# Expert lookup of a diffusion block: dots and sums of the gathered tokens in alternating groups of eight, and the dense tokens' routing earlier

## The chip, the cores and the metric

One Trainium2 chip, of which the program uses one core. The metric is device time in microseconds (us): 1965.21 us, the median of 3 runs (1963.86 to 1965.46). All data are float32.

## The reference, cut to what matters

The program is one layer of a diffusion backbone over 256 latent tokens of width 2048. After the mixers comes an expert feed-forward (PEER): every token picks 8 x 16 = 128 of 16,384 experts by two product keys, takes the dot of itself with each expert's row of `u_tab`, and sums the experts' rows of `v_tab` with gated weights.

```python
def peer_ffn(h, wq, keys, u_tab, v_tab):
    q = (ht @ wq).reshape(n, PEER_HEADS, 2, PEER_DK // 2)
    s = jnp.einsum('nhpc,pkc->nhpk', q, keys)
    s1, i1 = lax.top_k(s[:, :, 0], PEER_TOPK)
    s2, i2 = lax.top_k(s[:, :, 1], PEER_TOPK)
    cand = (s1[..., :, None] + s2[..., None, :]).reshape(n, PEER_HEADS, 256)
    sc, ci = lax.top_k(cand, PEER_TOPK)
    e = i1[ci // 16] * N_KEYS + i2[ci % 16]     # take_along_axis, shortened
    gate = jax.nn.softmax(sc, axis=-1)
    ...
        a = jnp.einsum('nd,nhkd->nhk', xb, jnp.take(u_tab, eb, axis=0))
        w = (gb * jax.nn.gelu(a)).astype(xb.dtype)
        return jnp.einsum('nhk,nhkd->nd', w, jnp.take(v_tab, eb, axis=0))
```

## The kernel before

The expert part treats the tokens in two ways. For 192 dense tokens (`NA`) the products with all 16,384 experts are computed on TensorE, in 128 steps of 128 experts; the wanted ones are picked afterwards. The other 64 gathered tokens (`NB`), two blocks of 32, have their own `u` rows fetched: one gather (an indirect DMA issued on POOL, 128 rows of 8 KB, 1 MB) brings 4 of a token's 128 experts for all 32 tokens of a block, so a block has 32 gathers of `u` rows and 32 of `v` rows. This makes 128 gathers. The dense tokens need 192 more, of `v` rows, after the dense stage: those are the tail.

**The dense stage.** A step loads 1 MB of `u_t` (SP), in two units of 1024 columns. Each unit is split by ACT into `hi` and by DVE into the rest `lo` (three buffers each, so that up to three units are prepared ahead), and TensorE does 8 pairs of matmuls `ups<-hf,hi` (384 columns) and `ups<-hf,lo` (192 columns). At the end of a step ACT copies `ut` out of PSUM and DVE adds it into the tile `W` (one `W<-ut,ups` on DVE is one step done). A `u_t` load needs a free wide buffer (the `wides` list).

**Gathered work beside it.** `gen_gather` walks a list `ops`. A `u` operation is a dot on DVE (`SCALAR_TENSOR_TENSOR ...<-...,hB`, 128x2048, with the sum in a column of `aB`), a `v` operation a sum on TensorE (four matmuls in the order, eight in the trace, into `adaps` for block 0 and `yb` for block 1, with weights `wB` that ACT scales). `fin` makes the weights out of the dots (GELU on ACT, times the gate on DVE); `hB` reloads one buffer with block 1's tokens from DRAM. Gathers are fetched in the list's order whenever a buffer of the list `gaths` is free. Buffers are lent out of `W`, whose later rows are not written yet: pieces 4, 6 and 8 of it for gathers, 1, 2, 3, 5, 7 and 9 for `u_t`, each taken back some steps before its row comes (piece i holds rows from 2048 i / 192 on). Pieces 10 and 11 hold the dense tokens' scores (`s0`) and scratch (`scr`).

**Order.** The code is written out unit by unit; after each one `pump()` advances side work ("lanes") whose due time in a model clock has come: a gather operation every `GP` = 4.65 us of that clock, and the lane `score` with the routing of block 1 of 128 tokens (it holds the gathered ones), a pause of `RT_DELAY`, and the routing of block 0 (dense tokens only): eight `score_top` (two top-16 searches each), four `pair_top`, the lookups `gen_look`, then `gen_route`. At step `RT_AT`, `open_px` completes what is left of that lane, forms the dense tokens' gather indices `eA`, and opens one more wide buffer and one more gather buffer in the space that the routing's tiles leave. Each engine executes its own list in order; only semaphores tie them.

Lines in the profile: every DVE and ACT instruction shows L132, every matmul L353 except the transposes `it` of the routing (L1276), gathers L1362, `u_t` loads L267, the reload of `hB` L1413.

Of the kernel before, what the change touches and what calls it, by code (L numbers as in the profile page):

```python
# [40 lines left out]
NK = 128  # L41
# [33 lines left out]
NA2 = 2  # L75
ADAY = 20.0
LAG = 3.0
UTB = 3
RT_AT = 104
RT_DELAY = 170.0  # L80
GP = 4.65
NAF = 2
GY = 8.0
# [94 lines left out]
def build(tc, a, stack, dbg=None):  # L178
# [851 lines left out]
    gaths = Slots(lambda u: u.used, 2048)  # L1030

    LENT_U = (1, 2, 3, 5, 7, 9)
    LENT = (4, 6, 8)
    x1d = tc.dram_tile([P, KD, T], F32, name="x1_spill")

    def make_hf(u):
        drain(only=("ada",))
        x1 = Y["x"]
        ss = mm_ps("ss1")
        mm(ss[:, 0:T], ones, Y["sq"], start=True, stop=False)  # L1040
        mm(ss[:, 0:T], ones, Y["last"], start=False, stop=True)
        prepare()
        rs = con.tile([P, T], F32, name="rs1", tag="rs1")
        rstd_of(rs, ss[:, 0:T], D)
        araws.drop(V["B"])
        close_pool(V["pb"])
        R["rh"] = open_pool("rh", side="right")
        R["rsb"] = open_pool("rsb", side="right")
        R["rs"] = open_pool("rs", side="right")
        H, S, SB = R["rh"][1], R["rs"][1], R["rsb"][1]  # L1050
        hf = H.tile([P, KD, 2, T], F32R, name="hf", tag="hf")
        hB = H.tile([P, D], F32, name="hB", tag="hB")
        R.update(hB=hB, hf=hf, hfs=hf.rearrange("p k s t -> p s k t"))
        R["keys"] = S.tile([P, 2, NK], F32, name="keys")
        sync.dma_start(R["keys"], a["keys"])
        sync.dma_start(x1d, x1)
        dump("x1", x1)
        n2 = 2 * PH * TOPK
        R["val"] = SB.tile([P, 2, n2], F32, name="val")
        R["ix"] = SB.tile([P, 2, n2], U32, name="ix")  # L1060
        R["sc"] = SB.tile([P, PH, TOPK], F32, name="sc")
        R["ci"] = SB.tile([P, PH, TOPK], U32, name="ci")
        R["e12"] = SB.tile([P, 3, PH, TOPK], F32, name="e12")
        R["h64"] = S.tile([P, KD, NB], F32, name="h64")
        shift, hm = mod[:, 3, 0], {}

        def scaled(k):
            hm[k] = S.tile([P, T], F32, name="hm1", tag="hm1", bufs=4)
            vec.scalar_tensor_tensor(hm[k], x1[:, k], gm[:, 2, k:k + 1], rs, op0=OP.mult, op1=OP.mult)

        skew(KD, scaled,
             lambda k: act.activation(hf[:, k, 0], hm[k], AF.Identity, bias=shift[:, k:k + 1]),
             lambda k: vec.scalar_tensor_tensor(hf[:, k, 1], hm[k], shift[:, k:k + 1],
                                                hf[:, k, 0].bitcast(F32), op0=OP.add, op1=OP.subtract))
        spawn("hA", copy_hB())

        close_pool(pa)
        R["w"] = open_pool("w")
        R["W"] = R["w"][1].tile([P, NK, NA], F32, name="W")
        flat = R["W"].rearrange("p e n -> p (e n)")  # L1080
        room = [flat[:, c * 2048:(c + 1) * 2048] for c in range(NK * NA // 2048)]
        R["scr"] = room.pop()
        R["s0"] = room.pop().rearrange("p (h k) -> p h k", k=NK)
        for i in LENT_U:
            wides.place(("row", i), room[i], i * 2048 // NA - 3)
        for i in LENT:
            gaths.place(("lent", i), room[i])

    hBd = tc.dram_tile([P, D], F32, name="hB_spill")
# [143 lines left out]
    def gen_route(blk, rp):  # L1233
        if blk == 1:
            it = con.tile([P, 1152], F32, name="iT", tag="st")
            R["iT"] = it[:, 0:3 * T].rearrange("p (s t) -> p s t", s=3)
            R["eA"] = it[:, 3 * T:3 * T + NA].bitcast(I32)
            R["idx"], R["gB"], R["aB"] = (
                it[:, c:c + 2 * STEPS].rearrange("p (b s) -> p b s", b=2)
                for c in range(3 * T + NA, 1152, 2 * STEPS))  # L1240
            R["idx"] = R["idx"].bitcast(I32)
            ib = con.tile([P, 2 * T], BF16, name="ib", tag="rs1")
            R["i1b"], R["idb"] = ib[:, 0:T].rearrange("p (b c) -> p b c", b=2), ib[:, T:T + P]
            vec.tensor_copy(R["idb"], ident)
        yield from gen_look(blk, 1, rp)
        sc, e12 = R["sc"], R["e12"]
        sm, e = R["scr"][:, 0:PH], R["scr"][:, 16:16 + P]

        vec.tensor_copy(sm, sc[:, :, 0])
        vec.tensor_tensor(sc, sc, sm[:, :, None].to_broadcast([P, PH, TOPK]), op=OP.subtract)  # L1250
        act.activation(sc, sc, AF.Exp)
        e12f = e12.rearrange("p s h j -> p s (h j)")
        if blk == 1:

            lo = P - NB
            vec.scalar_tensor_tensor(e[lo:P], e12f[lo:P, 0], float(NK), e12f[lo:P, 1], op0=OP.mult, op1=OP.add)
            for g in range(2):
                for r in range(REP):
                    vec.tensor_copy(R["idx"][r * BT:(r + 1) * BT, g],
                                    e[lo + g * BT:lo + (g + 1) * BT, r * STEPS:(r + 1) * STEPS])  # L1260
            spawn("gather", gen_gather())
        vec.tensor_copy(R["i1b"][:, blk], e12f[:, 0])
        yield 1.0
        vec.tensor_reduce(sm, sc, axis=mybir.AxisListType.X, op=OP.add)
        vec.reciprocal(sm, sm)
        vec.tensor_tensor(e12[:, 2], sc, sm[:, :, None].to_broadcast([P, PH, TOPK]), op=OP.mult)
        dump(f"e12_{blk}", e12f)
        if blk == 1:
            for g in range(2):
                for r in range(REP):  # L1270
                    vec.tensor_copy(R["gB"][r * BT:(r + 1) * BT, g],
                                    e12f[P - NB + g * BT:P - NB + (g + 1) * BT, 2, r * STEPS:(r + 1) * STEPS])
        yield ITY
        pt = sm_ps("it")
        for s in range(3):
            ten.transpose(pt[:, s * P:(s + 1) * P], e12f[:, s], ident)  # L1276
        act.activation(R["iT"][:, 0:3, blk * P:(blk + 1) * P], pt[:, 0:3 * P].rearrange("p (s t) -> p s t", s=3),
                       AF.Copy)
        yield 0.0
# [40 lines left out]
    def open_px(u):  # L1320
# [6 lines left out]
        wides.add(R["px"][1], "raw", F32, 1)  # L1327
        gaths.add(R["px"][1], "gath", F32, 1)

    for i, tag in enumerate(("rawA", "rawB")):  # L1330
        wides.take_over(pipe, tag, lambda i=i: all(s[3] is None or raws.done(s[3]) for s in raws.slots[2 * i:2 * i + 2]))
    add(None, False, open_w)
# [49 lines left out]
    def gen_gather():  # L1382

        aB, n = R["aB"], STEPS
        ops = [("u", 0, s) for s in range(n)] + [("fin", 0, 0), ("v", 0, 0), ("hB", 1, 0), ("v", 0, 1)]
        for s in range(n):
            ops += [("u", 1, s)] + [("v", 0, s + 2)] * (s + 2 < n)
        ops += [("fin", 1, 0)] + [("v", 1, s) for s in range(n)]
        for kind, b, s in ops:
            if kind in ("u", "v"):  # L1390
                to_get.append((a[kind + "_rows"], R["idx"][:, b, s:s + 1]))
        scaled = {}

        def scale(b, s):
            w = scaled[b, s] = R["t"][1].tile([P, BT], F32, name="wB", tag="wB", bufs=2)
            act.activation(w, selb, AF.Copy, scale=aB[:, b, s:s + 1])

        fetch()
        yield 4.0
        for j, (kind, b, s) in enumerate(ops):  # L1400
            if kind == "v" and b == 1 and s == 0:
                to_get.extend((a["v_rows"], R["eA"][:, t:t + 1]) for t in range(NA))
            if kind == "fin":
                act.activation(aB[:, b], aB[:, b], GELU)
                vec.tensor_tensor(aB[:, b], aB[:, b], R["gB"][:, b], op=OP.mult)
                YB[b] = ada_ps() if b == 0 else sm_ps("yb")
                yield 2.0
                scale(b, 0)
                yield 2.0
                continue  # L1410
            if kind == "hB":
                R["hB"] = R["rh"][1].tile([P, D], F32, name="hB", tag="hB")
                sync.dma_start(R["hB"], hBd)  # L1413
                continue
            fetch()
            g = got.popleft()
            if kind == "u":
                vec.scalar_tensor_tensor(g.raw, g.raw, 1.0, R["hB"], op0=OP.mult, op1=OP.mult,
                                         accum_out=aB[:, b, s:s + 1])
                g.used = True  # L1420
            else:
                add_rows(YB[b], scaled.pop((b, s)), g, s == 0, s == n - 1)
                if s + 1 < n:
                    scale(b, s + 1)
            fetch()
            yield GP
# [312 lines left out]
```

## Time and profile before

| | |
|---|---|
| median of 3 runs | 1965.21 us |
| the profiled execution's own time | 1964.57 us |
| its span, first to last instruction | 1962.8 us |
| TensorE busy, mean granted clock | 1724.8 us (88%), 0.943 |
| VectorE (DVE) busy | 1224.6 us (62%) |
| ScalarE (ACT) busy | 700.6 us (36%) |
| GpSimd (POOL) busy | 376.6 us (19%) |
| moved by DMA | 670.20 MB, mean 341 GB/s |

Times inside the program are counted from the span's start. The dense stage's 128th step ends at about 1451 us; the stretch from 834 us (14 steps done) to there is what the change touches, and the tail runs from there to 1962.8 us. A busy share is an average over stages, so the stage's own windows are read first, and then what ended the waits in them. TensorE's matmuls are pipelined: it counts as busy also where it runs at the lower clock.

### The profile page before, as it was taken

To read this page: it belongs to the slowest core of one execution; us is meant where nothing else is said; L and a number is where in the kernel's file an instruction comes from. 1 tells how busy PE (TensorE), PEld (TensorE's weight loads), DVE (VectorE), ACT (ScalarE), POOL (GpSimd) and SP (SyncE) were. 2 spreads that over 40 slices of the span, in tenths; PEclk is the share of its full clock that TensorE was granted. 3 is DMA by queue.
4 is the path that set the end of the run, shared out by engine and by line. 5 is a ranking of instruction groups with operands and counts; after the bars stand their busy time and mean duration, and the time that the engine had idled before them with its cause. 6 is when DMAs were issued, how large, how long until landed. Compare 5 with 4: busy or idle time off the path is not lost.

```text
span 1962.8 us, 29973 instructions
## 1 busy us (share of the span) xinstructions
PE 1724.8 (88%) x11882; PEld 1362.9 (69%) x11882; DVE 1224.6 (62%) x2492; ACT 700.6 (36%) x1099; POOL 376.6 (19%) x324
## 2 busy tenths in 40 slices
PE   4999999999899999899899998999987666776775
PEld 2689789879798898899888887888853222222221
DVE  5256868776798669899689996764434323323232
ACT  4235335555543544455444443444421001001000
POOL 0000000000000000333222322223333333333331
PEclk8999999999899999999999999999998998889886
DMA  9975878776698764999999999899989999999996
GB/s 396 368 272 183 287 240 306 275 250 208 198 334 297 262 202 137 422 420 420 373 367 390 387 395 350 338 382 406 380 343 421 421 421 421 421 420 421 420 421 282
DMA packets 115869, 670.20 MB, mean 341 GB/s; under 512 B 12688, under 2 KB 15248, under 8 KB 53264
## 3 DMA queue, kind: packets, MB, share of 16 engines
q1 hardware_dynamic: 69648, 332.72, 45.9%
q0 software_dynamic: 46080, 335.56, 41.7%
q8 instruction: 93, 1.52, 0.3%
q14 instruction: 48, 0.39, 0.1%
HBM read 662.99 MB, written 5.24 MB: 340 GB/s over the span
## 4 chain that ended last, share of the span: by engine, by line
PE 60%; DMA 27%; issue 7%; DVE 4%; ACT 1%; POOL 1%; SPq 0%; POOLq 0%; ACTq 0%; DVEq 0%
PE mm L353 25%; PE ups L353 22%; DMA gath<-in_v_rows,iT 14%; DMA hB<-in_v_rows,iT 2%; PE y L353 2%; PE adaps L353 2%; DMA rawB<-in_v_rows,iT 2%; DMA rawA<-in_v_rows,iT 2%; DMA ring<-in_ada 2%; DMA raw<-in_v_rows,iT 2%; PE sm L353 1%; PE num L353 1%; PE yb L353 1%; DVE lo L132 1%; DMA rawA<-in_u_t 1%
## 5 line engine op out<-in xcount | busy, mean ns | idle before, releaser
L353 PE MATMUL ups<-hf,hi 128*128 128x384 f32 x2048 | 605.3, 368 | 0.0
L353 PE MATMUL ups<-hf,lo 128*128 128x192 f32 x2048 | 516.9, 252 | 16.5 <-DVE lo L132 16.5
L353 PEld LDWEIGHTS ups<-hf,hi 128*128 128x128 f32 x2048 | 389.0, 190 | 51.6 <-issue 43.6
L353 PEld LDWEIGHTS ups<-hf,lo 128*128 128x128 f32 x2048 | 395.6, 193 | 19.3 <-DVE lo L132 19.1
L132 DVE TENSOR_TENSOR lo<-rawA,hi 128x1024 fp32r<-128x1024 f32 x146 | 178.3, 1221 | 118.3 <-ACT hi L132 103.8
L132 DVE TENSOR_TENSOR lo<-rawB,hi 128x1024 fp32r<-128x1024 f32 x144 | 175.7, 1222 | 111.1 <-ACT hi L132 105.0
L132 DVE SCALAR_TENSOR_TENSOR oh<-c,iT,pick 128x128 f32<-128x128 f32 x192 | 55.3, 344 | 298.8 <-PE pick L353 298.8
L1362 POOL DMA_INDIRECT gath<-in_v_rows,iT x134 | 157.1, 1172 | 321.0 <-PE y L353 125.8
L132 ACT ACTIVATE hi<-rawA 128x1024 fp32r<-128x1024 f32 x146 | 154.2, 1056 | 173.1 <-PE ups L353 79.0
L1362 POOL DMA_INDIRECT W<-in_u_rows,iT x28 | 45.1, 1611 | 872.4 <-DMA W<-in_u_t 781.5
L132 ACT ACTIVATE hi<-rawB 128x1024 fp32r<-128x1024 f32 x144 | 152.0, 1057 | 155.1 <-PE ups L353 65.0
L353 PE MATMUL mm<-xL,hi 128*128 128x256 f32 x864 | 181.1, 290 | 4.8 <-ACT xL L132 1.7
L132 ACT ACTIVATE hi<-W 128x1024 fp32r<-128x1024 f32 x106 | 112.4, 1060 | 148.5 <-PE ups L353 143.3
L353 PEld LDWEIGHTS mm<-xL,hi 128*128 128x128 f32 x864 | 144.0, 192 | 14.2 <-issue 7.5
L132 DVE SCALAR_TENSOR_TENSOR adacc<-araw,early,adacc 128x1024 f32<-128x1024 f32 x120 | 152.3, 1277 | 0.0
L353 PE MATMUL y<-gath,wA 128*32 128x512 f32 x648 | 100.6, 701 | 56.7 <-DMA gath<-in_v_rows,iT 56.7
L132 ACT ACTIVATE uA<-uA 128x4 f32<-128x4 f32 x48 | 9.9, 205 | 385.7 <-DVE oh L132 385.7
L132 DVE TENSOR_TENSOR lo<-W,hi 128x1024 fp32r<-128x1024 f32 x106 | 128.4, 1218 | 23.5 <-ACT hi L132 23.1
L353 PE MATMUL mm<-xL,lo 128*128 128x256 f32 x432 | 122.5, 284 | 0.0
L353 PEld LDWEIGHTS pick<-W,oh 128*128 128x128 f32 x384 | 79.4, 255 | 57.8 <-issue 56.3
L353 PE MATMUL mm<-hf,hi 128*128 128x256 f32 x512 | 98.1, 290 | 6.7 <-ACT hf L132 5.3
L353 PE MATMUL pick<-W,oh 128*128 128x128 f32 x384 | 97.9, 412 | 0.7 <-issue 0.7
(278 smaller groups left out, 2871.8 us busy)
## 6 DMA issues: line engine op xcount, KB each, us to landing
araw<-in_ada SPq DMA_DIRECT2D x128, 512.0 KB, 5.1
W<-in_u_t SPq DMA_DIRECT2D x53, 1024.0 KB, 9.4
rawB<-in_u_t SPq DMA_DIRECT2D x34, 1024.0 KB, 9.2
rawA<-in_u_t SPq DMA_DIRECT2D x34, 1024.0 KB, 9.7
ring<-in_ada SPq DMA_DIRECT2D x32, 1024.0 KB, 12.1
rawB<-in_wout SPq DMA_DIRECT2D x16, 512.0 KB, 5.8
rawA<-in_wout SPq DMA_DIRECT2D x16, 512.0 KB, 6.1
rawB<-in_wq SPq DMA_DIRECT2D x16, 512.0 KB, 4.0
```

What stands on the lines that cost most here:

```text
L132: return f(*args, **kw)
L353: ten.matmul(out, lhsT, rhs, start=start, stop=stop, skip_group_check=True, **kw)
L1362: pool.indirect_dma_start(out=g.raw, out_offset=None, in_=tab, in_offset=bass.IndirectOffsetOnAxis(ap=idx, axis=0))
```

## The change

The list `ops` is ordered anew. Before: all 32 dots of block 0, `fin`, its sums mixed with block 1's dots, `fin`, block 1's sums. Now, in each block: dot `s` followed by sum `s - 8`, a `fin` for eight columns after every eighth dot, the last eight sums at the block's end. `hB` is reloaded after the second of block 0's last eight sums. `fin` waits in the model for the gates. The dense tokens' routing starts after 60 instead of 170 us of the model's clock, and `open_px` stands at step 66 instead of 104. It now also lends pieces 10 (to `u_t`, until row 103) and 11 (to gathers, taken back before row 117). The counts of dots, sums, gathers and loads stay; there are 8 `fin` instead of 2.

```diff
+SUB = 8
-RT_AT = 104
-RT_DELAY = 170.0
+RT_AT = 66
+RT_DELAY = 60.0
...
-    LENT = (4, 6, 8)
+    LENT = (4, 6, 8, 11)
...
-        R["scr"] = room.pop()
-        R["s0"] = room.pop().rearrange("p (h k) -> p h k", k=NK)
+        R["room"], R["scr"] = room, room[11]
+        R["s0"] = room[10].rearrange("p (h k) -> p h k", k=NK)
...
-        for i in LENT:
+        for i in LENT[:-1]:
...
+            R["gates"] = True
...
+        wides.place(("row", 10), R["room"][10], 10 * 2048 // NA - 3)
+        gaths.place(("lent", 11), R["room"][11])
...
-        ops = [("u", 0, s) for s in range(n)] + [("fin", 0, 0), ("v", 0, 0), ("hB", 1, 0), ("v", 0, 1)]
-        for s in range(n):
-            ops += [("u", 1, s)] + [("v", 0, s + 2)] * (s + 2 < n)
-        ops += [("fin", 1, 0)] + [("v", 1, s) for s in range(n)]
+        ops = []
+        for b in range(2):
+            for s in range(n):
+                ops += [("u", b, s)] + [("v", b, s - SUB)] * (s >= SUB)
+                if s % SUB == SUB - 1:
+                    ops.append(("fin", b, s + 1 - SUB))
+            ops += [("v", b, s) for s in range(n - SUB, n)]
+
+        ops.insert(ops.index(("v", 0, n - SUB)) + 2, ("hB", 1, 0))
...
-            if kind == "v" and b == 1 and s == 0:
+            if kind == "v" and b == 1 and s == n // 2:
...
-                act.activation(aB[:, b], aB[:, b], GELU)
-                vec.tensor_tensor(aB[:, b], aB[:, b], R["gB"][:, b], op=OP.mult)
-                YB[b] = ada_ps() if b == 0 else sm_ps("yb")
+                while "gates" not in R:
+                    yield 1.0
+                some = slice(s, s + SUB)
+                act.activation(aB[:, b, some], aB[:, b, some], GELU)
+                vec.tensor_tensor(aB[:, b, some], aB[:, b, some], R["gB"][:, b, some], op=OP.mult)
+                if s == 0:
+                    YB[b] = ada_ps() if b == 0 else sm_ps("yb")
                 yield 2.0
-                scale(b, 0)
-                yield 2.0
+                scale(b, s)
+                yield 0.0
...
-                if s + 1 < n:
+                if (s + 1) % SUB:
                     scale(b, s + 1)
```

Three places show what this does to the engines' lists. The first is SP, the queue of the loads, where `hB` is reloaded; numbers in names grow in the order in which the program was written out. Before:

```order
L267 DMA rawA_9180<-in_u_t 128x2048
L267 DMA W_5949<-in_u_t 128x2048 x3
L267 DMA rawB_9376<-in_u_t 128x2048
L1413 DMA hB_9418<-hB_spill_96 128x2048
L267 DMA rawA_9432<-in_u_t 128x2048
```

Now:

```order
L268 DMA rawB_10744<-in_u_t 128x2048
L268 DMA rawA_10799<-in_u_t 128x2048
L1427 DMA hB_10817<-hB_spill_96 128x2048
L268 DMA W_5949<-in_u_t 128x2048
L268 DMA raw0_10900<-in_u_t 128x2048
```

Before, the last dot that reads the old `hB` stands in step 39 of DVE's list, the reload in step 41, the first dot with the new one in step 42. Now they stand in steps 60, 64 and 69, with block 0's last sums between.

The second is DVE, where the dense tokens' `score_top` (MAX, MAX_INDEX, MATCH_REPLACE) meets a dot (`...,hB`). Before, steps 46 and 47:

```order
L132 TENSOR_TENSOR lo_9578<-W,hi_9576 128x1024
L132 MAX val<-W 128x8 x2
L132 MAX_INDEX ix<-val,W 128x8 x2
L132 MATCH_REPLACE W<-val,W 128x128 x2
L132 MAX val<-W 128x8 x2
L132 MAX_INDEX ix<-val,W 128x8 x2
L132 TENSOR_TENSOR lo_9617<-rawB,hi_9615 128x1024
L132 TENSOR_TENSOR W<-ut,ups 128x192
L132 TENSOR_TENSOR lo_9641<-rawB,hi_9639 128x1024
L132 SCALAR_TENSOR_TENSOR gath_9451,iT<-gath_9451,hB 128x2048
L132 TENSOR_TENSOR lo_9666<-rawA,hi_9664 128x1024
```

Now, step 20:

```order
L133 TENSOR_TENSOR lo_8365<-rawA,hi_8363 128x1024
L133 TENSOR_TENSOR W<-ut,ups 128x192
L133 MAX val<-W 128x8 x2
L133 MAX_INDEX ix<-val,W 128x8 x2
L133 MATCH_REPLACE W<-val,W 128x128 x2
L133 MAX val<-W 128x8 x2
L133 MAX_INDEX ix<-val,W 128x8 x2
L133 SCALAR_TENSOR_TENSOR gath_8161,iT<-gath_8161,hB 128x2048
L133 TENSOR_TENSOR lo_8402<-rawA,hi_8400 128x1024
L133 TENSOR_TENSOR lo_8424<-W,hi_8422 128x1024
```

The search and the dot stood two `lo` apart; now they stand side by side between two `lo`, in steps 20, 22, 24, 26 and 28, and a `pair_top` beside a dot in 38, 40 and 42. In the other steps a `lo` stays between.

The third is DVE at the end of the dense tokens' routing, where `e` (gates) is what TensorE's `it` transposes. Before, steps 94 to 96:

```order
L132 COPY W<-sc 128x8
L132 TENSOR_TENSOR sc<-sc,W 128x128
L132 CAST ib<-e_5879 128x128
L132 SCALAR_TENSOR_TENSOR gath_12121,iT<-gath_12121,hB 128x2048
L132 TENSOR_TENSOR lo_12232<-rawB,hi_12230 128x1024
L132 TENSOR_TENSOR W<-ut,ups 128x192
L132 TENSOR_REDUCE W<-sc 128x8
L132 RECIPROCAL W<-W 128x8
L132 TENSOR_TENSOR e_5879<-sc,W 128x128
L132 TENSOR_TENSOR lo_12259<-rawB,hi_12257 128x1024
```

Now, between steps 65 and 66:

```order
L133 TENSOR_REDUCE e_5879<-W 128x64
L133 TENSOR_TENSOR W<-ut,ups 128x192
L133 COPY W<-sc 128x8
L133 TENSOR_TENSOR sc<-sc,W 128x128
L133 CAST ib<-e_5879 128x128
L133 TENSOR_REDUCE W<-sc 128x8
L133 RECIPROCAL W<-W 128x8
L133 TENSOR_TENSOR e_5879<-sc,W 128x128
L133 SCALAR_TENSOR_TENSOR iT<-iT 128x192
L133 TENSOR_TENSOR lo_10905<-W,hi_10903 128x1024
```

`open_px` writes the whole rest of the routing out at one place. On TensorE the transposes `it` stood after step 95, more than a unit behind `e`; now they stand right after step 65's last matmul.

## Rows read from the trace of the kernel before

**Rows 1.** Windows: stretch, length, PE, PEld, DVE, ACT, POOL busy (count), clock, DMA share, GB/s.
```profile
834.00:952.20 118.20, 118.20 (x827) 118.20 (x826) 117.83 (x126) 60.67 (x79) 38.05 (x23) 1.00 1.01 420
952.20:1000.60 48.40, 41.46 (x270) 36.34 (x269) 28.89 (x46) 19.43 (x30) 9.81 (x8) 0.89 0.89 355
1000.60:1164.00 163.40, 163.40 (x1140) 147.38 (x1139) 153.06 (x351) 76.94 (x111) 44.99 (x32) 1.00 0.96 385
1164.00:1320.80 156.80, 144.97 (x971) 128.53 (x970) 108.63 (x132) 67.34 (x99) 38.04 (x28) 0.97 0.93 359
1320.80:1451.50 130.70, 130.70 (x911) 104.77 (x910) 58.63 (x66) 55.57 (x91) 42.58 (x25) 1.00 0.95 373
1451.50:1962.80 511.30, 353.57 (x2196) 136.86 (x2192) 160.68 (x728) 41.28 (x90) 183.36 (x194) 0.85 0.98 407
```

**Rows 2.** Windows, tile ut on DVE: the count is of steps done.
```profile
750.00:834.00 84.00, 4.83 (x14) 0.96 0.75 300
952.20:1000.60 48.40, 2.43 (x7) 0.89 0.89 355
1000.60:1164.00 163.40, 11.05 (x32) 1.00 0.96 385
1164.00:1320.80 156.80, 9.00 (x26) 0.97 0.93 359
1320.80:1451.50 130.70, 7.99 (x23) 1.00 0.95 373
```

**Rows 3.** Windows, tile wB on TensorE: matmuls of the sums, eight to a sum.
```profile
952.20:1000.60 48.40, 5.04 (x32) 0.89 0.89 355
1000.60:1164.00 163.40, 17.05 (x128) 1.00 0.96 385
1164.00:1320.80 156.80, 16.20 (x112) 0.97 0.93 359
1320.80:1451.50 130.70, 27.54 (x208) 1.00 0.95 373
```

**Rows 4.** Timeline of TensorE around 1005 us: start, length, instruction.
```profile
1004.98 0.25 PE L353 MATMUL ups<-hf,lo 128*128 128x192 f32 x1
...
1007.27 0.25 PE L353 MATMUL ups<-hf,lo 128*128 128x192 f32 x1
```

**Rows 5.** The chain of waits in 952:1000.5: start, length, what.
```profile
959.83 14.62 DMA hB<-hB_spill
```

**Rows 6.** Who waited for whom, 1164:1320.8: total, times, longest.
```profile
ACT hi L132 <- DMA rawB<-in_u_t: 21.0, 7, 7.2
...
PE adaps L353 <- DMA gath<-in_v_rows,iT: 10.4, 5, 4.5
```

**Rows 7.** Timeline of DVE around a score_top and a dot.
```profile
1001.53 0.48 DVE L132 MAX8 val<-W 128x8 f32<-128x128 f32 x2
...
1003.88 1.21 DVE L132 TENSOR_TENSOR lo<-W,hi 128x1024 fp32r<-128x1024 f32 x1
1005.00 0.35 DVE L132 TENSOR_TENSOR W<-ut,ups 128x192 f32<-128x192 f32 x1
...
1007.12 2.28 DVE L132 SCALAR_TENSOR_TENSOR W<-W,hB 128x2048 f32<-128x2048 f32 x1
```

**Rows 8.** Groups by line and shape on ACT and DVE: busy, mean ns.
```profile
L132 ACT ACT_TABLE_LOAD x4 | 5.1, 1283 | 0.1
...
L132 ACT ACTIVATE sc<-sc 128x128 f32<-128x128 f32 x2 | 0.6, 310 | 3.2 <-DVE sc L132 3.2
...
L132 DVE TENSOR_TENSOR e<-sc,W 128x128 f32<-128x128 f32 x1 | 0.3, 292 | 0.0
```

**Rows 9.** Timeline of TensorE at 794 us: in brackets the idle time before.
```profile
793.89 0.53 PE L353 MATMUL ups<-hf,lo 128*128 128x192 f32 x1 [4.20 <-DVE lo L132]
```

**Rows 10.** Window around that wait, all engines.
```profile
786.00:796.00 10.00, 4.99 (x27) 4.73 (x28) 6.63 (x8) 2.19 (x4) 5.14 (x4) 0.84 1.01 426
```

**Rows 11.** DMA packets in 834:1451.5.
```profile
DMA packets 32198, 234.70 MB, mean 380 GB/s; under 512 B 3583, under 2 KB 3583, under 8 KB 3583
```

## The prediction

> **What bounds the kernel now.** I read the windows of all engines first, then the same windows for the tiles that count steps and sums, then who waited for whom where TensorE is not busy throughout, and last the timeline around single instructions.
>
> The tail is bound by transfers: 194 gathers of 1.05 MB in 511.3 us at 407 GB/s [rows 1], and 420 GB/s is what a stretch shows when it is full. The change leaves it alone, except for how many gathers it has to take.
>
> In the dense stage TensorE is the bound, with two holes. A unit of eight matmul pairs takes 1007.27 - 1004.98 = 2.29 us [rows 4], a step 4.58 us. A sum costs what the full stretches leave over: (163.4 - 32 x 4.58) / 16 = 1.05 and (130.7 - 23 x 4.58) / 26 = 0.98 [rows 1 to 3]; I take 1.0. From 834 us, 114 steps and the 60 sums of the four later stretches (480 matmuls) would need 522.1 + 60 = 582.1 us; they took 617.5. The holes are where it is lost:
> - 952.2 to 1000.6: 7 steps and 4 sums are 36.1 us, it took 48.4: 12.3 lost. TensorE idles 6.9, and the clock is 0.89 [rows 1]. The chain names the reload of hB, 14.62 us [rows 5]: DVE stands at block 1's first dot until it has landed, and the `lo` behind that dot wait with it.
> - 1164 to 1320.8: 26 steps and 14 sums are 133.1 us, it took 156.8: 23.7 lost. ACT waits for `u_t` and TensorE, in its own list, for a gathered `v` row, 10.4 us [rows 6]. Here only two or three buffers are left for loads and two for gathers; the routing's space is opened at step 104.
>
> That is 36.0 us; the other stretches run 0.6 shorter than the formula.
>
> **The change part by part.**
> *The hB hole.* The reload now stands four steps after the last dot that reads the old tokens and five steps (over 23 us) before the first that reads the new. 14.62 us fit into that, so the 12.3 go. If that cover were gone, the same hole would come back once.
> *The buffer hole.* From step 66 there are five or six load buffers and five gather buffers, four of each around step 100, and three of each at the end, as many as before in 1320.8 to 1451.5, where TensorE was busy throughout [rows 1]. The 23.7 go, and what is late next is the last stretch, below.
> *Sums and dots.* Their counts stay. By the order of TensorE's list 7 sums instead of 5 stand behind the last step, so 58 instead of 60 in the stretch: -2.0. The two gathers they read move into the tail: 2 x 1.05 MB at 420 GB/s = +5.0 there. Eight `fin` instead of two are short, and they stand an operation behind their last dot; with sums in between they cost TensorE nothing, by the cover of `hi` and `lo` prepared ahead. Without it each would cost the 1.28 us of a table load at most, and by the order only two of them need one, as before.
> *Search and dot side by side, steps 20 to 42.* Behind a `score_top` alone (1001.53 to 1003.88, 2.35 us) the next `lo` ended at 1005.09 and its first matmul came at 1007.27 [rows 4, 7]: 2.18 us to spare. Now a dot (2.28) and a `W` addition (0.35) stand in front of it too. DVE starts an instruction some 0.09 us before the end of the one ahead (1.21 us from 1003.88, the next at 1005.00), so 2.28 + 0.35 - 2 x 0.09 - 2.18 = 0.27, about 0.3 us late, eight times: +2.4. Bounds: nothing, if the transfers delay TensorE anyway, and the whole dot, 8 x 2.2 = 17.6, if nothing was to spare. I take the row's own 0.3.
> *The routing's end, step 66.* `open_px` puts the transposes `it` right behind step 65, so TensorE stands while `ut`, the `W` addition, two short DVE instructions, a table load (1.28), the exponential (0.31) and three more short ones of about 0.3 [rows 8] follow one another: the table load can start behind `ut`, and I count 0.3 + 1.3 + 0.3 + 3 x 0.3 and small change = 3 us. TensorE's clock may fall on top: after 4.20 us of waiting [rows 9] the window shows 0.84 over 10 us [rows 10], which is 3.2 us at 1.2 instead of 2.4 GHz, an estimate of at most that much again. Bounds 0 (the work done beforehand) and 3 + 3.2 = 6.2; I take 4.5, nearer the upper, because only the clock's part is doubtful.
> *Nine steps of dots only (69 to 77).* No sums, so TensorE asks for a load and a gather (2.1 MB) every 4.58 us, while 420 GB/s give them every 5.0: 9 x 0.4 = 3.6 us, less what the extra buffers have fetched ahead in the eight steps of sums before. 0 to 3.6; I take 2.
> *The last 24 steps.* From step 104 three load buffers again, with TensorE faster than before: 4.58 + 0.5 per step against 5.68 (130.7 / 23). The demand is 2.1 MB in 5.1 us, 411 GB/s of 420. Nearest rows: none lost with three and three at 5.68; 23.7 / 26 = 0.91 us a step with two and three. So 0 to 22; I take 6, nearer the first because the number of buffers is the same.
>
> Sum for the stretch: 522.1 + 58 + 2.4 + 4.5 + 2 + 6 = 595.0 us, so the dense stage ends at 834 + 595 = 1429.0 instead of 1451.5: -22.5. With +5.0 in the tail: -17.5. The profiled execution took 1964.57 us (span 1962.8), which makes 1947.1; the runs' median is 0.6 above it, so 1948 us.
>
> Is there room on the transfers? The stretch moved 234.70 MB [rows 11]; two gathers less are 232.6 MB, at 420 GB/s 554 us of the 595. The Trainium skill ("DMA: Bandwidth & Descriptors", section "Where 436 GB/s comes from") says that for transfers from HBM into SBUF the HBM side binds at about 358 GB/s per core. The trace does not agree: 420 GB/s over 118 us [rows 1]. By that rule the stretch could not be shorter than 650 us and the result would be near 2002 us; it is the last rival below.
>
> **The rivals.**
> *Slower: the transfers take over.* With dots and sums both asking, loads share the engines with gathers from step 79 on, and each load buffer comes too late by what it did in the buffer hole, 0.91 us a step: 49 x 0.91 = 44.6 instead of 6. It decides as soon as a load's wait for its turn is longer than the two units that are prepared ahead (4.6 us). 1948 + 38.6 = 1987 us. For it: ACT waited 21.0 us for one of the load buffers alone [rows 6], and the demand is 98% of what flows. Against it: 1000.6 to 1164 ran at 385 GB/s with dots, sums and four, then three load buffers and lost nothing. 10%.
> *No change: the routing moves its cost.* DVE is busy 153.1 of 163.4 us where routing and dots meet [rows 1]; if each of the eight places costs its whole dot, 17.6 instead of 2.4, it comes to 1948 + 15.2 = 1963 us, the same as before within what can be told. Against it: the 2.18 us to spare. 11%.
> *More: none of the new waits shows.* 1948 - 14.9 = 1933 us. For it, the last stretch of before lost nothing; against it, TensorE has nothing else to do at step 66. 12%.
> *The rule of 358 GB/s.* 2002 us, 1%, as the 420 GB/s stand against it.
>
> **How the numbers follow.** The forecast has 66%. Its own range is 1937 to 1960: the last steps between 0 and 15, the rest with half their bounds. To hold 8 in 10 I go up to the second rival, 1966, and down to 1936. A measurement of this kernel tells about 0.2% (4 us) from no change. Faster by more: the forecast, the third rival and a little of the second, 0.79. Within 0.2%: most of the second, 0.09. Slower: the first, the fourth and the rest of the second, 0.12.
>
> **What would show it.** No wait on hB and no stretch with TensorE at 0.89 near step 64; in the steps 79 to 104 no wait of `adaps` for a gather, and steps of 5.1 us; eight waits of TensorE for `lo` of some 0.3 us in steps 20 to 42; one wait of about 3 us before the transposes `it`; the dense stage's last step near 1429 us; 196 gathers behind it and a tail of about 516 us. I am wrong if ACT's waits for `u_t` fill the last 49 steps and TensorE waits behind them, if the side-by-side places cost more than 1 us each, or if the tail grows by more than the two gathers.

## The result and the profile after

The changed kernel takes 1946.63 us (median of 4 runs, 1945.05 to 1947.18), the kernel before beside it 1965.34 us: a ratio of 0.9897, 95% interval 0.9876 to 0.9917. The forecast was 1948 us. The profiled execution took 1945.05 us, span 1943.3, against 1964.57 and 1962.8.

The windows of all engines after: stretch, length, PE, PEld, DVE, ACT, POOL busy (count), clock, DMA share, GB/s. The edges are starts of steps: 14, 65, 67, 80 and 107, then the last `W` addition.

```profile
827.40:1094.70 267.30, 266.97 (x1850) 238.42 (x1849) 233.92 (x465) 127.96 (x188) 75.73 (x49) 1.00 0.98 392
1094.70:1112.40 17.70, 15.09 (x88) 11.95 (x84) 8.31 (x14) 6.20 (x11) 7.00 (x5) 0.81 1.01 412
1112.40:1176.60 64.20, 64.20 (x450) 60.21 (x448) 53.67 (x58) 33.70 (x46) 20.25 (x12) 1.00 1.00 407
1176.60:1315.70 139.10, 139.10 (x973) 126.08 (x969) 99.94 (x108) 64.98 (x95) 44.90 (x26) 1.00 0.99 392
1315.70:1425.80 110.10, 110.10 (x770) 98.23 (x768) 75.91 (x85) 50.15 (x76) 33.31 (x20) 1.00 0.94 370
1425.80:1943.30 517.50, 351.75 (x2212) 134.30 (x2208) 160.92 (x728) 41.91 (x92) 184.94 (x196) 0.87 0.98 407
```

Both holes of [rows 1] are gone: from step 67 on TensorE is busy throughout. One stretch of 17.7 us has a low clock, 0.81, and TensorE idle in it. The tail has 196 gathers instead of 194.

**How the losses are counted here.** Cutting windows at round times and counting finished steps, as the prediction did, leaves up to a step of error at each edge. More exact is the time from the first matmul of a step to the first of a later one. The timeline of TensorE after, start, length, instruction, shows the first matmuls of steps 70 and 71 (dots only), and of 98, 99 and 100 with one sum between:

```profile
1129.66 0.36 PE L354 MATMUL ups<-hf,hi 128*128 128x384 f32 x1
...
1134.25 0.36 PE L354 MATMUL ups<-hf,hi 128*128 128x384 f32 x1
...
1269.67 0.44 PE L354 MATMUL ups<-hf,hi 128*128 128x384 f32 x1
...
1274.34 0.36 PE L354 MATMUL ups<-hf,hi 128*128 128x384 f32 x1
...
1279.02 1.06 PE L354 MATMUL yb<-gath,wB 128*32 128x512 f32 x8
1280.01 0.44 PE L354 MATMUL ups<-hf,hi 128*128 128x384 f32 x1
```

A step is 1134.25 - 1129.66 = 4.59 us (4.587 over many), two steps and a sum 1280.01 - 1269.67 = 10.34. So a sum costs 10.34 - 2 x 4.587 = 1.16 us, not 1.0. "Lost" below is what a stretch takes beyond 4.587 a step and 1.16 a sum, from such starts:

| stretch of steps | lost before | lost after |
|---|---|---|
| 14 to 39 | 0.0 | 1.5 |
| 40 to 79 (before: reload of hB; after: step 65 and 66) | 10.0 | 6.6 |
| 80 to 106 (before: the buffer hole) | 18.2 | 0.2 |
| 107 to the end | -0.3 | -0.4 |
| from step 14 to TensorE's last dense matmul | 619.9 us, 59.5 sums | 597.6 us, 57.5 sums |

(One sum lies across the end in both and is counted as half; the negative numbers are the error of that cut.) The dense stage is 22.3 us shorter; the forecast said 22.5.

TensorE's timeline around the transposes `it`, after (in brackets the idle time before an instruction, and what ended it):

```profile
1100.53 0.48 PE L1278 MATMUL it<-c,e 128*128 128x128 f32 x2
1103.62 0.48 PE L1278 MATMUL it<-c,e 128*128 128x128 f32 x1 [2.61 <-DVE e L133]
1103.75 0.67 PE L354 MATMUL ups<-hf,hi 128*128 128x384 f32 x1
...
1108.24 1.85 PE L354 MATMUL adaps<-gath,wB 128*32 128x512 f32 x8
1110.02 0.45 PE L354 MATMUL ups<-hf,hi 128*128 128x384 f32 x1
```

The transposes wait 2.61 us for `e`. Then a unit takes 1108.24 - 1103.75 = 4.49 us instead of 2.29, and from a sum to the matmul behind it (1110.02 - 1108.24) it is 1.78 instead of 0.99 (1280.01 - 1279.02 above). The window there, same columns as above, shows a granted clock of 0.51, the lower of the two levels (1.2 instead of 2.4 GHz):

```profile
1103.60:1110.00 6.40, 6.38 (x25) 4.54 (x25) 2.25 (x3) 2.70 (x4) 2.47 (x2) 0.51 1.02 429
```

Steps 65 and 66 lose 6.2 us in all: 2.6 of waiting, 3.0 of slow clock, the rest the transposes themselves.

Where a search and a dot stand side by side (DVE, then TensorE, step 21 after):

```profile
862.24 2.27 DVE L133 SCALAR_TENSOR_TENSOR gath<-gath,hB 128x2048 f32<-128x2048 f32 x1
864.44 0.08 DVE L133 DVE_READ_ACCUMULATOR gath<-gath,hB 128x1 f32 x1
864.44 1.22 DVE L133 TENSOR_TENSOR lo<-rawA,hi 128x1024 fp32r<-128x1024 f32 x1
```

```profile
865.33 0.36 PE L354 MATMUL ups<-hf,hi 128*128 128x384 f32 x1
865.72 0.36 PE L354 MATMUL ups<-hf,lo 128*128 128x192 f32 x1
865.92 0.35 PE L354 MATMUL ups<-hf,hi 128*128 128x384 f32 x1
866.11 0.25 PE L354 MATMUL ups<-hf,lo 128*128 128x192 f32 x1
866.20 0.36 PE L354 MATMUL ups<-hf,hi 128*128 128x384 f32 x1
```

`lo` ends at 865.66, the matmul on it starts at 865.72. From one `hi` matmul to the next it is 0.59 us instead of the usual 0.28: 0.3 lost, at six of the eight places, too short for a row of its own among the waits. The lesson: such losses are seen in the distance between like instructions.

### The profile page after: what moved, and what is told of

Read it like the earlier page. It is cut to its first block, busy times and chain, and to the rows that moved or that the text cites. A ratio compares the mean times of both kernels' runs of the same rounds, so it can differ in the third digit from the quotient of the medians.

```text
span 1943.3 us, 29970 instructions
## 1 busy us (share of the span) xinstructions
PE 1713.3 (88%) x11882; PEld 1354.1 (70%) x11882; DVE 1226.5 (63%) x2498; ACT 702.1 (36%) x1105; POOL 384.2 (20%) x324
## 4 chain that ended last, share of the span: by engine, by line
PE 68%; DMA 23%; DVE 4%; issue 3%; ACT 1%; POOL 0%; SPq 0%; POOLq 0%; ACTq 0%; DVEq 0%
PE ups L354 29%; PE mm L354 25%; DMA gath<-in_v_rows,iT 8%; DMA hB<-in_v_rows,iT 5%; DMA raw<-in_v_rows,iT 3%; PE adaps L354 3%; PE y L354 2%; DMA rawB<-in_v_rows,iT 2%; DMA ring<-in_ada 2%; DMA rawA<-in_v_rows,iT 2%; PE pick L354 1%; PE num L354 1%; PE yb L354 1%; PE sm L354 1%; PE pc L354 1%
## 5 line engine op out<-in xcount | busy, mean ns | idle before, releaser
L133 DVE TENSOR_TENSOR lo<-rawA,hi 128x1024 fp32r<-128x1024 f32 x134 | 163.7, 1223 | 103.7 <-ACT hi L133 95.4
L133 DVE TENSOR_TENSOR lo<-rawB,hi 128x1024 fp32r<-128x1024 f32 x132 | 161.3, 1222 | 92.3 <-ACT hi L133 88.4
L1367 POOL DMA_INDIRECT W<-in_u_rows,iT x24 | 37.7, 1570 | 847.0 <-DMA W<-in_u_t 778.4
L133 ACT ACTIVATE hi<-rawA 128x1024 fp32r<-128x1024 f32 x134 | 141.6, 1057 | 147.8 <-PE ups L354 73.8
L1367 POOL DMA_INDIRECT gath<-in_v_rows,iT x119 | 135.1, 1136 | 270.6 <-PE y L354 119.0
L133 ACT ACTIVATE hi<-rawB 128x1024 fp32r<-128x1024 f32 x132 | 139.4, 1057 | 130.3 <-PE ups L354 64.6
L133 ACT ACTIVATE hi<-W 128x1024 fp32r<-128x1024 f32 x114 | 120.8, 1060 | 149.7 <-PE ups L354 146.7
L133 DVE TENSOR_TENSOR lo<-W,hi 128x1024 fp32r<-128x1024 f32 x114 | 138.7, 1221 | 42.5 <-ACT hi L133 37.4
L354 PE MATMUL y<-gath,wA 128*32 128x512 f32 x664 | 96.7, 660 | 64.2 <-DMA gath<-in_v_rows,iT 61.5
L354 PEld LDWEIGHTS y<-gath,wA 128*32 128x32 f32 x664 | 13.8, 111 | 121.0 <-DMA gath<-in_v_rows,iT 107.9
```

The source lines that it names most:

```text
L133: return f(*args, **kw)
L354: ten.matmul(out, lhsT, rhs, start=start, stop=stop, skip_group_check=True, **kw)
L1367: pool.indirect_dma_start(out=g.raw, out_offset=None, in_=tab, in_offset=bass.IndirectOffsetOnAxis(ap=idx, axis=0))
```

## The experiments

Each kernel is the changed one with the edit shown, unless it says otherwise. Ratios are against the kernel before, run beside it.

**1. The order alone.** Routing and space as before.

```diff
-RT_AT = 66
-RT_DELAY = 60.0
+RT_AT = 104
+RT_DELAY = 170.0
-    LENT = (4, 6, 8, 11)
+    LENT = (4, 6, 8)
...
-        wides.place(("row", 10), R["room"][10], 10 * 2048 // NA - 3)
-        gaths.place(("lent", 11), R["room"][11])
```

> The new order of dots and sums alone; the dense tokens' routing, step 104 and the lent places as before. Theory (two separate holes): the 10.0 us that TensorE lost around the reload of hB go, two sums less stand in the dense stage (-2.3), the tail takes two gathers more (+6), and the 18.2 us of steps 81 to 106 stay: 1965.3 - 6.3 = 1959 us. Rival 1 (the order itself made the second hole): that goes too, 1941 us. Rival 2 (the holes are one shortage that only moves): 1965 us, with a larger loss in steps 81 to 106.

Measured: 1964.69 us (1959.13 to 1973.46), ratio 0.9989 (0.9967 to 1.001): no gain that can be told. Its windows, steps 14 to 67, 68 to 79 and 80 to 109:

```profile
831.40:1115.20 283.80, 283.80 (x1979) 252.78 (x1977) 227.90 (x444) 135.67 (x201) 93.42 (x53) 1.00 0.99 395
1115.20:1180.40 65.20, 59.46 (x405) 55.51 (x401) 61.02 (x81) 28.70 (x41) 18.28 (x11) 1.00 0.90 348
1180.40:1353.40 173.00, 161.28 (x1086) 143.62 (x1083) 119.51 (x134) 75.17 (x110) 40.75 (x31) 0.97 0.95 367
```

TensorE's own waits in 1115.2:1353.4:

```profile
PE yb L354 <- DMA gath<-in_v_rows,iT: 8.4, 5, 2.5
PE ups L354 <- DVE lo L133: 7.7, 9, 1.0
```

The hole at `hB` is gone, and steps 80 to 109 lose 18.1 as the theory said. But steps 68 to 79 lose 7.8: there a dot stands in every step, the routing still runs beside it, and TensorE waits for DVE's `lo`. DVE is busy 61.0 of 65.2 us. That was not expected.

**2. The routing alone.** The old order of dots and sums, with its two `fin`; the cut shows the list.

```diff
-        for b in range(2):
-            for s in range(n):
-                ops += [("u", b, s)] + [("v", b, s - SUB)] * (s >= SUB)
...
+        ops = [("u", 0, s) for s in range(n)] + [("fin", 0, 0), ("v", 0, 0), ("hB", 1, 0), ("v", 0, 1)]
+        for s in range(n):
+            ops += [("u", 1, s)] + [("v", 0, s + 2)] * (s + 2 < n)
+        ops += [("fin", 1, 0)] + [("v", 1, s) for s in range(n)]
...
```

> The routing sooner, with step 66 and the lent places as in the changed kernel, but the old order of dots and sums. Theory (two separate holes): the 18.2 us of steps 81 to 106 go, the 10.0 us at the reload of hB stay, the end of the routing costs 6.2 as in the changed kernel and five places where search and dot stand side by side 0.35 each: 1965.3 - 18.2 + 6.2 + 1.8 = 1955 us. Together with the order alone that gives the whole change. Rival (the holes depend on one another): less than 5 us gained, 1960 or more, since with all dots of a block in one row the buffers that come free are asked for at other times.

Measured: 1972.33 us (1968.35 to 1977.44), ratio 1.0031 (1.0015 to 1.0046): slower than before. Windows of steps 14 to 19, 20 to 43, 44 to 49, and 67 to the end:

```profile
827.10:854.70 27.60, 27.60 (x195) 27.60 (x194) 27.60 (x31) 14.02 (x18) 10.09 (x6) 1.00 1.01 418
854.70:989.60 134.90, 120.37 (x787) 113.82 (x785) 129.10 (x317) 58.20 (x77) 34.40 (x20) 0.97 0.90 351
989.60:1029.50 39.90, 34.88 (x227) 30.00 (x225) 32.90 (x51) 15.89 (x24) 10.73 (x7) 0.91 0.87 334
...
1122.30:1454.70 332.40, 332.40 (x2318) 287.19 (x2318) 203.54 (x221) 152.19 (x229) 105.08 (x63) 1.00 0.97 382
```

Steps 44 to 49, at the reload of hB, lose 7.7 us, and steps 62 to 67, at the routing's end, 5.5. From step 67 on nothing is lost: the buffer hole goes by the routing's part alone. But steps 20 to 43 take 134.9 us; in the kernel before the same steps with as many sums took 970.73 - 858.32 = 112.4. That is 22.5 us more. TensorE's own waits in 827:1455, then the window of the same steps before, and in the changed kernel:

```profile
PE ups L354 <- DVE lo L133: 19.5, 14, 5.0
```

```profile
858.30:970.70 112.40, 112.40 (x786) 110.40 (x785) 101.31 (x109) 58.16 (x77) 33.70 (x20) 1.00 1.01 420
```

```profile
858.40:984.50 126.10, 125.77 (x869) 112.23 (x866) 116.82 (x305) 57.69 (x85) 35.05 (x24) 1.00 0.96 383
```

In steps of dots alone DVE is busy all the time (27.60 of 27.60, first row) even without a search; [rows 1] already had that: 117.83 of 118.20 us. The searches add 129.10 - 101.31 = 27.8 us to DVE's busy time, and 22.5 of them come out as a delay of TensorE, which waits for `lo`. So the halves do not add up: -2.6 and +5.0 us alone by the medians, -18.7 together. The new order puts a dot into every second step only, and that is the room on DVE into which the early routing goes: in the changed kernel the same steps, with 12 sums instead of 2, have DVE busy 116.82 of 126.10 us and lose 2.1.

**3. Pieces 10 and 11 not lent.**

```diff
-    LENT = (4, 6, 8, 11)
+    LENT = (4, 6, 8)
...
-        wides.place(("row", 10), R["room"][10], 10 * 2048 // NA - 3)
-        gaths.place(("lent", 11), R["room"][11])
```

> The changed kernel without lending pieces 10 and 11 of W; only the two buffers in the routing's space come at step 66. Theory (three load and three gather buffers are enough for TensorE, as in the last stretch): no loss, 1946.6 us within 2. Rival (the lent places carry part of the gain): steps 94 to 104, which then have three and three instead of four and four, lose 0.7 us each as they did in the hole of before, 1954 us.

Measured: 1947.81 us (1947.29 to 1949.25), ratio 0.9905 (0.9879 to 0.9931), as the changed kernel. In a window that covers steps 94 to 104 TensorE is busy throughout; by starts, steps 94 to 106 lose 0.1 us. The lent places are worth nothing here.

```profile
1243.30:1310.00 66.70, 66.70 (x467) 60.70 (x466) 48.08 (x51) 31.80 (x46) 19.72 (x13) 1.00 0.98 388
```

**4. The routing 20 us sooner still.**

```diff
-RT_DELAY = 60.0
+RT_DELAY = 40.0
```

> The changed kernel with the pause before the dense tokens' routing 40 instead of 60 us of the model's clock: by the order the routing then ends by itself, its last e stands three units sooner in DVE's list than now, and the transposes at the same place in TensorE's; and no search stands beside a dot any more. Theory (the stall at step 66, its wait of 2.6 us and the slower clock behind it, 6.2 us in all, and six places of 0.35 us side by side are all that TensorE still loses): 1946.6 - 8.2 = 1938.4 us. Rival 1 (only the wait goes, the clock falls anyway): 1942 us. Rival 2 (the transfers set the pace, so what TensorE does sooner it waits for later): 1946 us.

Measured: 1940.07 us (1937.79 to 1943.69), ratio 0.9869 (0.9840 to 0.9898). The dense stage, then the tail:

```profile
827.40:1417.20 589.80, 589.80 (x4113) 532.61 (x4115) 471.23 (x728) 282.77 (x412) 174.81 (x112) 1.00 0.98 395
1417.20:1936.10 518.90, 359.83 (x2216) 137.13 (x2216) 161.05 (x729) 42.38 (x93) 183.91 (x196) 0.85 0.98 407
```

TensorE is busy 589.8 of 589.8 us at full clock and loses 0.2 us in 114 steps. The transfers did not stop it: rival 2 falls. So does rival 1 in this execution: the wait and the low clock went together. By the median alone, which lies between the theory and rival 1, the two can't be told apart.

**5. The space opened at step 70.**

```diff
-RT_AT = 66
+RT_AT = 70
```

> The changed kernel with the new space opened at step 70 instead of 66, so that the routing's last pieces come at their own due times and nothing of it is drained in one place; the eight places where search and dot stand side by side stay. Theory: the stall at step 66 with the slow clock behind it was 6.2 us, and the side-by-side places stay at 2.1: 1946.6 - 6.2 = 1940.4 us, about 2 more than a kernel without both. Rival 1 (only the wait counts): 1944 us. Rival 2 (buffers that come four steps later cost as much): 1946 us, with losses in steps 66 to 80.

Measured: 1943.77 us (1940.95 to 1945.81), ratio 0.9894 (0.9869 to 0.9918). The median lies at rival 1's 1944, and the four executions, from 1941 to 1946, part neither the theory from the rivals nor this kernel from the changed one. The profile, of the fastest of them, sides with the theory. The dense stage is 591.8 us long and loses 2.2 us, 2.1 of them in steps 20 to 43 where search and dot stand side by side (the changed kernel 2.1 there too); the 6.2 us at the routing's end are gone, and the clock is 1.00.

```profile
827.30:1419.10 591.80, 591.47 (x4113) 532.72 (x4115) 470.89 (x728) 282.43 (x412) 182.07 (x112) 1.00 0.98 394
```

**6. hB reloaded late.**

```diff
-        ops.insert(ops.index(("v", 0, n - SUB)) + 2, ("hB", 1, 0))
+        ops.insert(ops.index(("u", 1, 0)), ("hB", 1, 0))
```

> The changed kernel with the reload of hB moved from behind the second of block 0's last sums to right before block 1's first dot. Theory (the reload is hidden by the five steps ahead of it alone): TensorE idles again while DVE stands at the dot, the 10 us of before come back, 1956.6 us. Rival (the reload is hidden anyway, since the sums ahead of the dot leave lo prepared and SP's queue is short there): less than 3 us, 1946.6 to 1949 us.

Measured: 1956.74 us (1954.10 to 1959.72), ratio 0.9960 (0.9946 to 0.9974). The chain of waits in 1100:1145 (start, length, what) and the waits in 1080:1150:

```profile
1121.60 15.07 DMA hB<-hB_spill
```

```profile
DVE W L133 <- DMA hB<-hB_spill: 9.8, 1, 9.8
PEld ups L354 <- DVE lo L133: 8.8, 1, 8.8
```

DVE stands at the dot, the `lo` behind it stand with it, TensorE behind these. Steps 68 to 73 lose 11.7 us; the median is 10.1 above the changed kernel's. The theory holds: the early reload is worth the 10 us.

**7. Two load buffers from step 104 on.**

```diff
-        wides.add(R["px"][1], "raw", F32, 1)
```

> The changed kernel without the load buffer in the routing's space, so two instead of three load buffers from step 104 on, with three gather buffers. Theory A (the number of load buffers made the hole of before): 0.7 us a step as in steps 81 to 106 of before, 24 steps, 17 us: 1963 us. Theory B (it was the two gather buffers together with two or three loads): nothing, 1946.6 us. In between, about 8 us, if both count.

Measured: 1961.59 us (1956.10 to 1964.36), ratio 0.9982 (0.9968 to 0.9997). ACT's waits in 1302:1436.2, and the window:

```profile
ACT hi L133 <- DMA rawB<-in_u_t: 38.9, 9, 6.2
...
ACT hi L133 <- DMA rawA<-in_u_t: 17.9, 10, 4.4
```

```profile
1302.00:1436.20 134.20, 127.38 (x859) 112.29 (x858) 85.70 (x94) 55.42 (x85) 23.38 (x22) 0.99 0.92 349
```

The last 24 steps lose 11.3 us in the profile (0.47 a step), which is of the fastest of the ten executions; their median is 15 above the changed kernel's. Theory A, at somewhat less than its price. The transfers are not full here, 349 GB/s: what is short is a place to put a load.

**8. A gather operation every 4.45 us of the model's clock.**

```diff
-RT_DELAY = 60.0
-GP = 4.65
+RT_DELAY = 42.0
+GP = 4.45
```

> The changed kernel with a gather operation every 4.45 instead of 4.65 us of the model's clock and the pause before the routing 42 instead of 60: by the order no sum stands behind the last dense step any more (7 now), one search stands beside a dot, and the routing ends by itself. Theory (the dense stage's transfers have room): the tail loses the gathers of 7 sums at 2.64 us, 18.5 us; the dense stage gets 7 sums at 1.16, +8.1; the stall at step 66 and the side-by-side places go, -8: 1946.6 - 18.4 = 1928 us. Rival (the transfers are full and the gathers only move): the dense stage grows by what the tail loses, 1938.5 us.

Measured: 1929.53 us (1928.40 to 1932.41), ratio 0.9816 (0.9793 to 0.9839), as expected and the fastest of all. Two constants change at once here; the parts are read from the profile. Dense stage and tail:

```profile
831.50:1429.80 598.30, 598.27 (x4168) 533.89 (x4167) 471.03 (x726) 282.24 (x417) 193.46 (x120) 1.00 0.99 402
1429.80:1930.60 500.80, 346.56 (x2160) 134.77 (x2158) 160.76 (x729) 40.86 (x88) 176.60 (x189) 0.86 0.98 407
```

All 64 sums lie in the dense stage now: 114 x 4.587 + 64 x 1.16 + 1.2 lost = 598.3 us. The tail has 189 gathers and is 16.7 us shorter than in the changed kernel.

**9. Routing early, its space late.** The edits of 1, but with a pause of 40.

```diff
-RT_AT = 66
-RT_DELAY = 60.0
+RT_AT = 104
+RT_DELAY = 40.0
```

> New order, the dense tokens' routing early (pause 40, as in e4_early40), but the routing's space opened at step 104 and pieces 10 and 11 not lent, as before. It parts the routing's early start from the early space. Theory (in e1_order_alone the 7.8 us of steps 68 to 80 were DVE, which had searches beside a dot in every step, and the 18 of steps 80 to 110 the missing buffers): the first go, the second stay, 1940.1 + 18 = 1958 us. Rival (all 26 us are one shortage of buffers): steps 68 to 110 lose 26 again, 1965 us.

Measured: 1958.92 us (1952.97 to 1966.42), ratio 0.9966 (0.9944 to 0.9987). The median is the theory's. The profiled execution was one of the longer ones, 1965.91 us. In it steps 68 to 79 lose 2.4 instead of 7.8 us, but steps 80 to 109 lose 20.9. Two windows, each some us wider than these steps; in the first DVE is busy 53.65 of 69.0 us:

```profile
1111.00:1180.00 69.00, 67.63 (x463) 62.35 (x463) 53.65 (x59) 31.98 (x45) 20.10 (x13) 1.00 0.96 375
1180.00:1354.00 174.00, 160.80 (x1071) 143.52 (x1070) 113.88 (x124) 72.12 (x106) 41.19 (x30) 0.96 0.94 363
```

So in this execution 5.4 of the 7.8 us went with the searches, but steps 68 to 109 lose 23.3 in all, nearer the rival's 26 than the theory's 18. The executions reach from 1953 to 1966 us and cover both, and the interval overlaps that of experiment 1. That the early routing without its space leaves the buffer hole is shown; how much of the 26 us was DVE stays open.

**10. Two gather buffers from step 79 on.** Load buffers as in the changed kernel.

```diff
-    LENT = (4, 6, 8, 11)
+    LENT = (4, 6, 8)
...
-        gaths.add(R["px"][1], "gath", F32, 1)
...
-        gaths.place(("lent", 11), R["room"][11])
```

> The changed kernel with the load buffers as they are (four, from step 104 three) but without the gather buffer in the routing's space and without piece 11: two gather buffers instead of three or four from step 79 on. It is the other half of e7_two_loads. Theory A (both kinds count in the hole of before, loads for 11 of its 18 us in 26 steps, gathers for the rest): 7 us in 26 steps, 49 steps here, +13: 1960 us, with TensorE waiting for gathered v rows. Theory B (with three loads two gathers are enough): 1946.6 us.

Measured: 1975.91 us (1966.75 to 1981.71), ratio 1.0043 (1.0024 to 1.0061), 29 us above the changed kernel. Its waits in 1170:1460 and a window from step 80 on:

```profile
PE yb L354 <- DMA gath<-in_v_rows,iT: 16.2, 8, 3.6
...
DVE gath L133 <- DMA gath<-in_u_rows,iT: 17.3, 8, 4.0
```

```profile
1179.00:1440.00 261.00, 242.92 (x1644) 217.93 (x1643) 170.61 (x185) 111.32 (x162) 69.77 (x45) 0.97 0.93 361
```

Steps 80 to 121 lose 25 us, 0.6 a step, with the full number of load buffers. So either shortage alone makes most of the hole of before (0.47 and 0.6 of 0.7 us a step), and the split of theory A, 11 for loads and 7 for gathers, is wrong: the two do not add up.

## Why the prediction was right, and where not

The total was right: 1948 forecast, 1946.63 measured. Its terms, for the profiled executions (losses by the starts of steps):

| term | predicted | measured | from |
|---|---|---|---|
| hole at hB | -12.3 | -10.0 | starts of steps 40 to 80; experiment 6 brings it back |
| buffer hole | -23.7 | -18.0 | starts of steps 80 to 107; experiments 7 and 10 |
| two sums less | -2.0 | -2.3 | 2 x 1.16 |
| side by side | +2.4 | +2.1 | six places of 0.3 to 0.4 |
| routing's end | +4.5 | +6.2 | steps 65 and 66; experiments 4 and 5 |
| steps of dots only | +2 | 0.0 | 4.59 a step, after |
| last 24 steps | +6 | 0.0 | after |
| tail | +5.0 | +6.2 | 518.3 - 512.1, behind TensorE's last dense matmul |

**The holes were there and went, as said, but were mis-sized.** The step that failed is the counting of whole steps between round times. By TensorE's own matmuls the four later windows of [rows 2] hold 7.38, 31.56, 26.69 and 21.91 steps, where 7, 32, 26 and 23 were counted. From the two full windows the sum came out at 1.0 instead of 1.16 us; in the two others the holes came out at 36.0 instead of 28.2. The rates taken from these counts are off too: a step of the last stretch took 130.7 / 21.91 = 5.97 us, not 5.68, and the hole lost 18.2 / 26.69 = 0.68 us a step, not 0.91. With a sum at 1.16, 114 steps and 57.5 sums need 589.6 us without any loss; the forecast had 580.1. This error was made good by two terms that did not come, together 8 us: the steps of dots only and the last 24 steps lose nothing. That the dense stage was right to 0.2 us is therefore luck. What was forecast as the reason stands: experiments 6, 7 and 10 each bring a hole back by taking one cover away.

**The steps of dots only and the last steps.** The prediction weighed the demand (411 of 420 GB/s) and feared the transfers. The changed kernel itself asked for less: 392 GB/s in steps 80 to 106 and 370 behind them. Experiments 4 and 8 come nearer the limit and lose next to nothing: 395 and 402 GB/s over the whole dense stage, 0.2 and 1.2 us lost. With three buffers of each kind the demand is met; what starves TensorE is a buffer less (experiments 7 and 10), at 349 and 361 GB/s. So the first rival, "the transfers take over", has the right mechanism only for two buffers. The fourth rival falls by the same rows: the Trainium skill ("DMA: Bandwidth & Descriptors", section "Where 436 GB/s comes from") has the HBM side binding at about 358 GB/s, a core's half of what a stack gives two; this program runs on one core, and experiment 8 shows 402 over 598.3 us. Of the third rival, that none of the new waits shows, half came true: these two terms are nothing, the next two are there.

**The routing's end.** In the profiled execution the wait, priced at 3, is 2.6; the clock's part was "at most 3.2" and is 3.0. The upper bound, 6.2, would have been the better choice for this execution; experiment 6 shows one in which the clock did not fall (last section).

**Side by side.** 0.27 us was worked out from the kernel before, 0.3 to 0.4 measured at six places; two lose nothing.

**The tail.** Two gathers at the tail's own mean, 511.3 / 194 = 2.64 us, are 5.3 of the 6.2 us. Where the other 0.9 goes was not tried.

**What the prediction did not see** is that the two halves need one another. It gave each hole a cause of its own, which holds for the whole change; experiments 1 and 2 show that alone the order gains nothing that can be told and the routing costs 0.31%. The second rival named the place (DVE, where routing meets dots) with 153.1 of 163.4 us [rows 1], but the fuller row, 117.83 of 118.20, was two lines above.

**Outside the change.** Step 14 starts at 830.8 us in the execution before and at 827.4 after. This is not the change: it starts near 827.3 in experiments 2, 4, 5, 6 and 7 and near 831.5 in 1, 3, 8, 9 and 10, and the program of experiment 3 is the changed kernel's up to there. So 3.4 of the 19.5 us between the two profiled executions are not the change's; its own part is -22.3 + 6.2 = -16.1, where -17.5 was forecast. The medians differ by 18.7; how much of that lies ahead of step 14 is not known, as only one execution of each has a profile. Here too the agreement of the totals is partly luck.

## What to carry to other kernels

Price a repeated piece of work from the start of one like instruction to the start of a later one, with a known count between, never from counts in windows with cut edges; a sixth of a microsecond on sixty sums was 10 us here. Before work is moved under another stage, read how full each engine is there in its own stage: 117.83 of 118.20 us says that next to nothing fits, whatever the mean says. And when a change has two halves, ask whether one makes the room that the other fills; then neither can be judged alone.

## What the runs showed of the hardware

After the same wait of 2.61 us for `e` the clock did not always fall. In the changed kernel the next 6.4 us ran at 0.51 of full speed (above). In experiment 6 the timeline of TensorE shows the same wait, and the window behind it the full clock; in experiment 3, whose program is the same up to there, it was 0.74:

```profile
1103.66 0.33 PE L1278 MATMUL it<-c,e 128*128 128x128 f32 x1 [2.61 <-DVE e L133]
```

```profile
1103.60:1110.00 6.40, 6.34 (x44) 5.35 (x45) 2.81 (x4) 2.99 (x5) 4.02 (x3) 1.00 1.01 426
```

```profile
1107.60:1114.00 6.40, 6.32 (x34) 5.32 (x35) 2.72 (x4) 2.70 (x4) 1.88 (x2) 0.74 1.01 426
```

Steps 62 to 67 lost 6.1 us in the first case, 3.2 in the second and 4.7 in the third; in experiments 7 and 10, with the same wait, 6.0. Here the stall cost its wait every time and the clock's part of up to 3 us not every time, so its price is a range. What decides was not tried.

The kernels that are short of buffers also scatter more: 1956 to 1964, 1953 to 1966 and 1967 to 1982 us in experiments 7, 9 and 10, with 10, 7 and 10 executions, against 1937.8 to 1943.7 in experiment 4 and 1928.4 to 1932.4 in 8, with 4 each. Why executions differ so there was not tried.
